# Sums of weights by transfers within DRAM ahead of their use, and token sums at an earlier step, in a two-level Strassen MLP

## The chip, the core and the metric

The kernel runs on one core of one Trainium2 chip. The metric is the device time of one execution in microseconds, the median of several runs. The core has five engines with an instruction queue each: PE (TensorE: matmul, with PEld for its weight loads), DVE (VectorE), ACT (ScalarE), POOL (GpSimd) and SP, which here only issues transfers. An engine works through its queue in order; an instruction that waits holds up all that is queued behind it. Transfers started by SP (queue q1 in the profile) and by POOL (queue q0) run on the core's 16 DMA engines. Transfers that add into their destination are started by POOL in this kernel.

## The reference, cut to what matters

One decoder block on 2048 tokens of width 1024, all in float32: attention and a gated unit side by side, merged, then an MLP. The change touches only the first matrix product of the MLP:

```
h = _rmsnorm(x, norm_pre_mlp)                        # 2048 x 1024
a = relu(einsum('bsd,df->bsf', h, w_mlp_in))         # w_mlp_in is 1024 x 4096
y = einsum('bsf,fd->bsd', a * a, w_mlp_out)
x = x + _rmsnorm(y, norm_post_mlp)
```

## The kernel before

Everything up to the MLP's normalised input `h2_d` (in DRAM) ends some 1390 us into the span. Then comes the first MLP stage (`hstep`, `hproduct`), up to about 2064 us, and the second (`yproduct`), up to the end.

**Two levels of seven products.** The first stage computes the product of the transposed weights (left) and the normalised tokens (right) with the Strassen-Winograd scheme in two levels: seven block products in place of eight, and each of them again split into seven. The outer level is a loop over the seven entries of `OUTER`, in the order A11, A12, S2, S1, S4, S3, A22: these are the left operands. The letters A11 to A22 are quarters of the weight matrix (rows by features, columns by depth), and

- S1 = A21 + A22
- S2 = S1 - A11
- S4 = A12 - S2
- S3 = A11 - A21 (the kernel before makes its negative, A21 - A11, and subtracts the product)

Each outer product runs over eight steps `q` (`HQ = 8`), so there are 56 steps `(o, q)` in `hsteps`, numbered `n`. A step takes 512 KB of left operand and makes seven inner products of six matmuls each (two blocks of depth, three matmuls each because float32 numbers are split in a high and a low part). That is 392 products; `yorder` lists them in order, and `k` counts them from 0, so an outer product spans 56 values of `k`. Products of neighbouring steps overlap a little in this order.

**What each engine does in a step.** SP loads the raw left operand (`load_ha`, line 1366). POOL makes the four inner sums of it (lines 1393, 1394, 1398, 1399 in `combine`), ACT rounds the parts to their high halves (1395, 1401, 1402, 1406), and DVE subtracts to get the low halves (1397, 1404, 1405, 1408). PE multiplies (1534). ACT or DVE evacuate PSUM to the accumulators `X` and the stage tiles `e` (1546 to 1552). SP stores finished tiles (`s_d`, `m5_d`). In the outer product S1 some tiles are added to `X` by a transfer that POOL starts (`collect`, 1567), and line 1579 takes them out again later.

**The order.** In this part the program's order is the order on each engine: after every product `k`, the entries of `todo[k]` that `later(k, ...)` has put there are issued. So `later` is the planner, by hand, and a number in it counts products. When the last product of step `n` is issued, the sums of step `n+3` are put at the next five products and the load of step `n+5` at the sixth; the sums that use this load start nine products after it.

**The left sums.** `TERMS` says of which terms a raw operand is made: S2 from A21, A22 and -A11; S1 from A21 and A22; S4 from A12 and -S2; S3 from A21 and -A11. The first term is loaded by SP into the buffer `hraw`, the second and third are added to the same buffer by accumulating transfers that POOL starts, three and six products after the load (line 1364). The negative of A11 and of S2 is made by ACT when that operand passes through (`negate`, 1379) and stored to DRAM by SP (`put`, 1384). There are two buffers `hraw`.

**The right operands.** For each outer product there are two tiles `w2r` of token blocks (`load_hb`, 1454), loaded at its predecessor's first step, eight blocks of 128x512 in all. For three of the outer products another block is subtracted from them first (`less_load` 1458, `less_sub` 1462, one of the two tiles on DVE, the other on POOL). Then `sum_w2` makes the inner sums T1, T3, T2 and T4 in place (lines 1484, 1485, 1487, 1489, twice each), and `op_w2`/`ops_hb` split the blocks into high and low parts ("spots", 1477 and the later-called subtractions that the profile books on line 1941). The two tiles are used again for the next outer product when the last split has read them.

Of the kernel before, what the change touches and what calls it, by code (L numbers as in the profile page):

```python
# [42 lines left out]
def block_kernel(ctx, tc, a, out):  # L43
# [90 lines left out]
    def dtile(shape, name):  # L134
        return dram.tile(shape, F32, name=name)
# [1210 lines left out]

    TERMS = dict(S2=("A21", "A22", "-A11"), S1=("A21", "A22"), S4=("A12", "-S2"), S3=("A21", "-A11"))

    def load_ha(n, term=0):
        o, q = hsteps[n]  # L1350
        terms = TERMS.get(OUTER[o][1], (OUTER[o][1],))
        if term >= len(terms):
            return
        name = terms[term]
        if not term:
            hraw_[n] = r4.tile([P, 4, 256], F32, name=f"hraw_{n}", tag="sraw", bufs=2)
        raw = hraw_[n].rearrange("p (f k) c -> p f (k c)", f=2)
        if name[0] == "A":
            f0, k0 = 2 * q + (16 if name[1] == "2" else 0), 4 if name[2] == "2" else 0
            src = a["w_mlp_in"][f0:f0 + 2, :, k0:k0 + 4].rearrange("f p k c -> p f (k c)")  # L1360
        else:
            src = neg_d[name[1:]][q]
        if term:
            pool.dma_start(raw, src, accum_op=OP.add)
        else:
            sp.dma_start(raw, src)

    def negate(n):

        o, q = hsteps[n]  # L1370
        name, raw = OUTER[o][1], hraw_[n]
        dst = neg_d[name][q].rearrange("p f c -> p (f c)")
        if name == "A11" and q > 1:
            z = [X[(0, 0, 8, 9, 12, 13, 14, 15)[q]]]
        else:
            z = [rx.tile([P, 512], F32, name=f"neg{n}{m}", tag="xs", bufs=4) for m in range(2)]
        w = D // len(z)
        for m, t in enumerate(z):
            act.activation(t, raw.rearrange("p k c -> p (k c)")[:, m * w:(m + 1) * w], AF.Copy, scale=-1.0)
        return [(dst[:, m * w:(m + 1) * w], t) for m, t in enumerate(z)]  # L1380

# [29 lines left out]
    def sum_ha(n):  # L1411
        w = hs_[n] = ring(n, f"hs_{n}", [P, 2, 7, 256])
        kept = negate(n) if OUTER[hsteps[n][0]][1] in neg_d else []
        yield from staged(combine(n, w, hraw_.pop(n)), kept)
# [53 lines left out]
    def key(o, m):  # L1468
        return m if o == 7 else (o, m)
# [9 lines left out]

    def sum_w2(q, part, eng=None):  # L1480

        r, e = w2r_[q], eng or pool
        if part == 0:
            e.tensor_sub(r[:, 4], r[:, 1], r[:, 0])
            e.tensor_sub(r[:, 1], r[:, 3], r[:, 1])
        if part in (1, 2):
            e.tensor_sub(r[:, 0], r[:, 3], r[:, 4])
        if part in (1, 3):
            e.tensor_sub(r[:, 2], r[:, 2], r[:, 0])
# [32 lines left out]
    def hproduct(k, n, i):  # L1522
# [22 lines left out]
        if m in (1, 5) and first:  # L1545
            act.activation(t, p, AF.Copy)  # L1546
        elif m in (2, 3) and first:
            dve.tensor_add(t, x_, p)
        elif m == 7:
            dve.tensor_sub(t, t, p)  # L1550
        else:
            dve.tensor_add(t, t, p)  # L1552
# [28 lines left out]
    def hstep(k, n, i):  # L1581
# [465 lines left out]
```

## Time and profile before

| | |
|---|---|
| median of 3 runs | 2691.23 us (2690.83 to 2695.79) |
| profiled execution | 2692.99 us, its span 2691.3 us |
| PE busy | 2580.0 us, 96% |
| first MLP stage | about 1390 to 2064 us |
| transfers of 512 KB that add into `hraw` (line 1364) | 40 |
| mean share of the DMA engines in the stage | 0.65 to 0.93 by outer product |

Engine times are busy times. A matmul's duration covers its way through the array and overlaps the next one's, so how fast PE goes is read from the distance of starts. "Idle before" is the time an engine stood before an instruction, with what released it. A wait is booked where the engine stood; what it waited for may itself have waited.

### The profile page before, as it was taken

Reading aid. Unit: us, or ns where it says so; the run is one execution under the profiler, and the core shown is the slowest. Engines: PE = TensorE matmul, PEld = TensorE weight load, DVE = VectorE, ACT = ScalarE, POOL = GpSimd, SP = SyncE. Lnnn points to the kernel's source line nnn. Section 1 sums busy time; section 2 is a strip of 40 time slices with the busy share of each in tenths; the row PEclk is TensorE's granted clock in tenths of the full one; section 3 lists DMA queues with packets and bytes.
Section 4 is the critical chain, followed back from the end, with each engine's and each line's share of the span. In section 5 each row is a group of like instructions: output and inputs, shape, how many; then the busy total and the mean of one; then the engine's idle time right before and its main releaser. Section 6 shows DMA issues by size and latency. Waiting matters only on the chain. (4 is left out here: it accounts for less than half of the span.)

```text
span 2691.3 us, 35656 instructions
## 1 busy us (share of the span) xinstructions
PE 2580.0 (96%) x12122; PEld 2140.5 (80%) x12122; DVE 1788.6 (66%) x3107; ACT 1110.7 (41%) x2342; POOL 1381.2 (51%) x1295
## 2 busy tenths in 40 slices
PE   9999999999999999999999968888899999999998
PEld 8888888888888877888887756767677888888887
DVE  5676574535434475765668756678678887788867
ACT  5213111254455445444355222433224555555555
POOL 0362354365364563101136456657698776777634
PEclk9999999999999999999999988999999999999999
DMA  8779778888888898645565786898976212222236
GB/s 318 279 246 325 269 228 291 298 278 264 295 269 239 239 319 313 224 157 180 181 240 198 199 207 141 223 250 195 263 239 190 84 52 92 88 87 86 87 110 211
DMA packets 419145, 568.70 MB, mean 211 GB/s; under 512 B 58897, under 2 KB 247569, under 8 KB 417938
## 3 DMA queue, kind: packets, MB, share of 16 engines
q1 hardware_dynamic: 386512, 491.09, 55.7%
q0 software_dynamic: 22560, 68.69, 9.9%
q10 hardware_dynamic: 9890, 6.62, 0.8%
q8 instruction: 96, 1.57, 0.2%
q14 instruction: 87, 0.71, 0.1%
HBM read 366.36 MB, written 195.76 MB: 209 GB/s over the span
## 5 line engine op out<-in xcount | busy, mean ns | idle before, releaser
L1534 PE MATMUL ha<-spot,hs 128*128 128x512 f32 x1344 | 351.8, 411 | 43.9 <-ACT e L1546 10.8
L1534 PEld LDWEIGHTS ha<-spot,hs 128*128 128x128 f32 x1344 | 266.0, 200 | 113.7 <-ACT e L1546 13.5
L1848 PE MATMUL ya<-spot,s 128*128 128x512 f32 x1344 | 324.1, 390 | 4.0 <-DVE X_yt L1856 2.1
L1848 PEld LDWEIGHTS ya<-spot,s 128*128 128x128 f32 x1344 | 252.2, 188 | 57.3 <-ACT spot L1477 2.5
L1534 PE MATMUL hc<-spot,hs 128*128 128x512 f32 x672 | 183.1, 410 | 40.7 <-DVE X_yt L1552 13.5
L1534 PEld LDWEIGHTS hc<-spot,hs 128*128 128x128 f32 x672 | 131.6, 198 | 75.9 <-DVE e L1552 12.9
L728 PE MATMUL g<-opA,spots 128*128 128x512 f32 x672 | 170.6, 398 | 1.8 <-DVE cv L760 1.8
L1848 PE MATMUL yc<-spot,s 128*128 128x512 f32 x672 | 170.5, 389 | 0.0
L728 PE MATMUL g<-opB,spots 128*128 128x512 f32 x648 | 164.6, 398 | 0.9 <-POOL spots L79 0.9
L96 PE MATMUL x<-hT_a,wq 128*128 128x512 f32 x384 | 149.7, 390 | 0.0
L97 PE MATMUL x<-hT_a,wq 128*128 128x512 f32 x384 | 149.4, 389 | 0.0
L98 PE MATMUL x<-hT_a,wq 128*128 128x512 f32 x384 | 149.4, 389 | 0.0
L1848 PEld LDWEIGHTS yc<-spot,s 128*128 128x128 f32 x672 | 126.1, 188 | 26.2
L728 PEld LDWEIGHTS g<-opA,spots 128*128 128x128 f32 x672 | 121.0, 188 | 23.9 <-issue 2.2
L79 POOL TENSOR_TENSOR spots<-gr,spots 128x512 fp32r<-128x512 f32 x98 | 128.7, 1317 | 20.8 <-DMA gr<-in_w_in_dram 7.0
L79 POOL TENSOR_TENSOR spot<-w2r,spot 128x512 fp32r<-128x512 f32 x79 | 112.3, 1444 | 45.3 <-ACT spot L71 45.3
L1712 ACT ACTIVATE sraw<-sraw 128x1024 f32<-128x1024 f32 x128 | 134.7, 1052 | 1.9 <-DMA sraw<-sd 0.2
L728 PEld LDWEIGHTS g<-opB,spots 128*128 128x128 f32 x648 | 116.7, 188 | 22.8 <-POOL spots L79 1.8
L71 ACT ACTIVATE hl<-r 128x512 fp32r<-128x512 f32 x48 | 30.4, 633 | 237.2 <-POOL r L329 89.0
L73 POOL TENSOR_SCALAR spots<-gr 128x512 fp32r<-128x512 f32 x86 | 55.4, 644 | 132.7 <-PE g L728 92.8
L978 DVE TENSOR_REDUCE o<-po 128x256 f32<-128x512 f32 x48 | 33.2, 692 | 133.9 <-PE po L977 133.9
L1397 DVE TENSOR_TENSOR hs<-hraw,hs 128x768 fp32r<-128x768 f32 x56 | 64.0, 1143 | 76.4 <-ACT hs L1395 76.4
(477 smaller groups left out, 6782.1 us busy)
## 6 DMA issues: line engine op xcount, KB each, us to landing
sraw<-sd SPq DMA_DIRECT2D x128, 256.0 KB, 3.3
hraw<-in_w_mlp_in_dram SPq DMA_DIRECT2D x56, 512.0 KB, 5.0
qk<-hl SPq DMA_DIRECT2D x24, 1024.0 KB, 5.7
qq<-qk SPq DMA_DIRECT2D x96, 256.0 KB, 5.1
sd<-e SPq DMA_DIRECT2D x64, 256.0 KB, 4.5
w2r<-in_w_mlp_out_dram SPq DMA_DIRECT2D x16, 1024.0 KB, 9.3
g<-gated SPq DMA_DIRECT2D x56, 256.0 KB, 4.9
gr<-sgd SPq DMA_DIRECT2D x53, 256.0 KB, 4.7
```

The costliest lines, as they stand in the source:

```text
L71: act.activation(hi, src, AF.Copy)
L73: pool.tensor_scalar(hi, src, 1.0, 1.0, op0=OP.mult, op1=OP.mult)
L79: (pool if lo_eng == "pool" else dve).tensor_sub(lo, src, f32(hi))
L96: pe.matmul(ps, lh, rh, start=start, stop=False)
L97: pe.matmul(ps, lh, rl, start=False, stop=False)
L98: pe.matmul(ps, ll, rh, start=False, stop=stop)
L728: pe.matmul(p, w[:, l, k], h[:, r, k], start=i in (1, 6, 5, 4) and not k and not m, stop=k == 3 and m == 2, skip_group_check=True)
L978: dve.tensor_reduce(ot[:, :, j * 64:(j + 1) * 64], po.rearrange("p (b h e) -> p b e h", b=4, h=2), axis=AX.X, op=OP.add)
L1397: dve.tensor_sub(lo[:, :3], raw[:, :3], f32(hi[:, :3]))
L1534: pe.matmul(p, w[:, l, S_AT[i], kk * P:(kk + 1) * P], b[r], start=i in (1, 2, 5) and not kk and not z, stop=kk == 1 and z == 2, skip_group ...
L1712: act.activation(sraw_[n], sraw_[n], func)
L1848: pe.matmul(p, s[:, l], w[r], start=i in (1, 2, 5) and not m and not o, stop=m == 1 and o == 2, skip_group_check=True)
```

## The change

Two things are changed, both in the first MLP stage.

The left sums are made in DRAM. There is now a DRAM tensor for each of S1, S2, S3 and S4. `negate` stores -A11 to the place of S2, and -S2 to the places of S4 and of S3. Accumulating transfers from the weights to these places (`add_rows`, started by POOL) complete them: S2 gets A21 and A22, S4 gets A12, S3 gets A22 (which makes A11 - A21, so the product is added now). S1 is first copied, A21 from DRAM to DRAM (`copy_rows`, started by SP), and then gets A22. All are placed at a fixed `k` by a loop over `q`. `load_ha` is one transfer for every operand.

The inner sums of the token blocks for the next outer product are placed from its predecessor's fourth step on (`q == 3`) in place of the sixth and seventh, with one tile on DVE and the other on POOL; T4 stays at the last step, one on each engine too. The early subtractions of `less_sub` come four products apart in place of five, the first a product earlier.

```
@@ dtile
-    neg_d = {name: dtile([NF // 4, P, 2, 512], f"neg{name}d") for name in ("A11", "S2")}
+    sums_d = {name: dtile([NF // 4, P, 2, 512], f"{name}d") for name in ("S1", "S2", "S3", "S4")}
@@ load_ha
-    TERMS = dict(S2=("A21", "A22", "-A11"), S1=("A21", "A22"), S4=("A12", "-S2"), S3=("A21", "-A11"))
+    def left_rows(name, q):
+        f0, k0 = 2 * q + (16 if name[1] == "2" else 0), 4 if name[2] == "2" else 0
+        return a["w_mlp_in"][f0:f0 + 2, :, k0:k0 + 4].rearrange("f p k c -> p f (k c)")
-        if term:
-            pool.dma_start(raw, src, accum_op=OP.add)
-        else:
-            sp.dma_start(raw, src)
+        raw = hraw_[n] = r4.tile([P, 4, 256], F32, name=f"hraw_{n}", tag="sraw", bufs=2)
+        sp.dma_start(raw.rearrange("p (f k) c -> p f (k c)", f=2), left_rows(name, q) if name[0] == "A" else sums_d[name][q])
+    def add_rows(name, q, term):
+        pool.dma_start(sums_d[name][q], left_rows(term, q), accum_op=OP.add)
+    def copy_rows(name, q, term):
+        sp.dma_start(sums_d[name][q], left_rows(term, q))
+    NEGATED = {"A11": ("S2",), "S2": ("S4", "S3")}
@@ negate
-        return [(dst[:, m * w:(m + 1) * w], t) for m, t in enumerate(z)]
+        return [(sums_d[to][q].rearrange("p f c -> p (f c)")[:, m * w:(m + 1) * w], t)
+                for to in NEGATED[name] for m, t in enumerate(z)]
@@
+    def sum_hb(q, name, eng):
+        to, x, y = {"T1": (4, 1, 0), "T3": (1, 3, 1), "T2": (0, 3, 4), "T4": (2, 2, 0)}[name]
+        r = w2r_[q]
+        eng.tensor_sub(r[:, to], r[:, x], r[:, y])
@@ hproduct
-        elif m == 7:
-            dve.tensor_sub(t, t, p)
@@ hstep
-                    later(k + 12 + 5 * m, less_load, o + 1, b)
+                    later(k + 11 + 4 * m, less_load, o + 1, b)
-                        later(k + 16 + 5 * m, less_sub, o + 1, b, kk)
+                        later(k + 15 + 4 * m, less_sub, o + 1, b, kk)
-        if i == 6 and q in (5, 6):
-            for w in range(2):
-                later(k + w, sum_w2, key(o + 1, w), 0 if q == 5 else 2, dve if not o else None)
+        if i == 6 and q == 3:
+            for m, part in enumerate(("T1", "T3", "T2")):
+                for w, eng in enumerate((dve, pool)):
+                    later(k + ((7, 11, 16) if o + 1 in LESS else (3, 8, 16))[m] + w, sum_hb, key(o + 1, w), part, eng)
-                    later(k + 3 + w, sum_w2, key(o + 1, w), 3)
+                    later(k + 3 + w, sum_hb, key(o + 1, w), "T4", (dve, pool)[w])
@@ before the loop over products
+        later(49 + 5 * q, add_rows, "S2", q, "A21")
+        later(60 + 5 * q, add_rows, "S2", q, "A22")
+        later(64 + 7 * q, copy_rows, "S1", q, "A21")
+        later(80 + 7 * q, add_rows, "S1", q, "A22")
+        later(162 + 7 * q, add_rows, "S4", q, "A12")
+        later(200 + 7 * q, add_rows, "S3", q, "A22")
@@ after the load of step m + 2
-                    if m + 2 < NH:
-                        later(k + 9, load_ha, m + 2, 1)
-                        later(k + 12, load_ha, m + 2, 2)
```

More of the change, by code (lines that the diff above doesn't have):

```diff
@@ L1345, in ring, with load_ha @@
         return (l3 if n % 3 == 2 else r4).tile(shape, F32R, name=name, tag=f"s{n % 3}")
-    TERMS = dict(S2=("A21", "A22", "-A11"), S1=("A21", "A22"), S4=("A12", "-S2"), S3=("A21", "-A11"))
-    def load_ha(n, term=0):
+    def left_rows(name, q):
+        f0, k0 = 2 * q + (16 if name[1] == "2" else 0), 4 if name[2] == "2" else 0
+        return a["w_mlp_in"][f0:f0 + 2, :, k0:k0 + 4].rearrange("f p k c -> p f (k c)")
+    def load_ha(n):
         o, q = hsteps[n]
[L1351 to L1360, printed above, removed]
-        else:
-            src = neg_d[name[1:]][q]
-        if term:
-            pool.dma_start(raw, src, accum_op=OP.add)
-        else:
-            sp.dma_start(raw, src)
+        name = OUTER[o][1]
+        raw = hraw_[n] = r4.tile([P, 4, 256], F32, name=f"hraw_{n}", tag="sraw", bufs=2)
[5 more added lines that the diff above has]
+    NEGATED = {"A11": ("S2",), "S2": ("S4", "S3")}
     def negate(n):
@@ L1371, in negate @@
         name, raw = OUTER[o][1], hraw_[n]
-        dst = neg_d[name][q].rearrange("p f c -> p (f c)")
         if name == "A11" and q > 1:
@@ L1412, in sum_ha @@
         w = hs_[n] = ring(n, f"hs_{n}", [P, 2, 7, 256])
-        kept = negate(n) if OUTER[hsteps[n][0]][1] in neg_d else []
+        kept = negate(n) if OUTER[hsteps[n][0]][1] in NEGATED else []
         yield from staged(combine(n, w, hraw_.pop(n)), kept)
@@ L1478, in ops_hb, with sum_w2 @@
             later(k + 1 + m, eng.tensor_sub, lo, src, f32(hi))
-    def sum_w2(q, part, eng=None):
-        r, e = w2r_[q], eng or pool
+    def sum_hb(q, name, eng):
+        to, x, y = {"T1": (4, 1, 0), "T3": (1, 3, 1), "T2": (0, 3, 4), "T4": (2, 2, 0)}[name]
+        r = w2r_[q]
+        eng.tensor_sub(r[:, to], r[:, x], r[:, y])
+    def sum_w2(q, part):
+        r, e = w2r_[q], pool
         if part == 0:
@@ L1485, in sum_w2 @@
             e.tensor_sub(r[:, 1], r[:, 3], r[:, 1])
-        if part in (1, 2):
+        else:
             e.tensor_sub(r[:, 0], r[:, 3], r[:, 4])
-        if part in (1, 3):
             e.tensor_sub(r[:, 2], r[:, 2], r[:, 0])
```

## The prediction

> **What bounds the kernel now.** I read the page first, then the waits, then the first MLP stage (1390 to 2064 us) product by product.
>
> ```profile
> span 2691.3 us, 35656 instructions
> PE 2580.0 (96%) x12122; PEld 2140.5 (80%) x12122; DVE 1788.6 (66%) x3107; ACT 1110.7 (41%) x2342; POOL 1381.2 (51%) x1295
> ...
> L1534 PE MATMUL ha<-spot,hs 128*128 128x512 f32 x1344 | 351.8, 411 | 43.9 <-ACT e L1546 10.8
> ...
> L1534 PE MATMUL hc<-spot,hs 128*128 128x512 f32 x672 | 183.1, 410 | 40.7 <-DVE X_yt L1552 13.5
> ```
>
> TensorE sets the time, and 84.6 us of its idle time of 111 stand before the products of this one stage (line 1534), behind evacuations of PSUM. The next rows cut the stage at its seven outer products, A11, A12, S2, S1, S4, S3, A22, which I call phases 0 to 6 (cut where the first evacuation of each form appears). The columns are the stretch, its length, the busy time of PE, PEld, DVE, ACT and POOL, the granted clock, the DMA engines' share, GB/s.
>
> ```profile
> 1390.00:1472.00 82.00, 79.73 (x356) 64.84 (x355) 65.48 (x93) 51.87 (x98) 46.55 (x45) 1.00 0.76 267
> 1472.00:1558.00 86.00, 78.75 (x330) 64.55 (x331) 68.14 (x95) 22.30 (x42) 44.44 (x46) 0.94 0.65 180
> 1558.00:1675.00 117.00, 87.43 (x316) 67.47 (x316) 67.52 (x95) 30.65 (x59) 63.79 (x64) 0.85 0.73 175
> 1675.00:1777.00 102.00, 88.77 (x365) 70.51 (x363) 73.52 (x89) 44.49 (x84) 74.67 (x72) 0.95 0.87 216
> 1777.00:1867.00 90.00, 81.39 (x336) 64.76 (x336) 70.82 (x101) 24.80 (x45) 57.30 (x58) 0.96 0.93 239
> 1867.00:1965.00 98.00, 83.63 (x335) 66.41 (x336) 69.87 (x99) 25.49 (x47) 69.94 (x65) 0.93 0.82 231
> 1965.00:2064.00 99.00, 85.71 (x352) 67.08 (x351) 78.13 (x104) 31.60 (x54) 93.79 (x79) 0.97 0.72 222
> ```
>
> Undisturbed, a product of six matmuls takes 1.36 us, so a phase of 56 products takes 76.2 us:
>
> ```profile
> 1429.22 1.52 PE L1534 MATMUL hc<-spot,hs 128*128 128x512 f32 x6
> 1430.58 1.52 PE L1534 MATMUL hb<-spot,hs 128*128 128x512 f32 x6
> ```
>
> Above that floor stand 10, 41, 26, 14, 22 and 23 us in phases 1 to 6: 136 us, idle time and the lower clock after it (0.85 in phase 2) together. No engine fills phase 2; it waits in a chain. The longest stall of it, in order of time:
>
> ```profile
> 1589.19 0.90 POOL L1364 DMA_DIRECT2D hraw<-negA11d  x1 [4.85 <-DMA hraw<-in_w_mlp_in_dram]
> 1596.65 1.15 ACT L1379 ACTIVATE neg<-hraw 128x512 f32<-128x512 f32 x2 [11.63 <-DMA hraw<-negA11d]
> 1598.56 0.96 DVE L1397 TENSOR_TENSOR hs<-hraw,hs 128x768 fp32r<-128x768 f32 x1 [10.43 <-ACT hs L1395]
> 1599.44 0.68 DVE L1552 TENSOR_TENSOR X_yt<-X_yt,hc 128x512 f32<-128x512 f32 x1
> 1600.17 2.93 PE L1534 MATMUL hc<-spot,hs 128*128 128x512 f32 x6 [9.53 <-DVE X_yt L1552]
> ```
>
> POOL stands 4.85 us until the second term has landed before it may issue the third, ACT waits for the third, DVE for ACT, and the evacuation that frees the PSUM bank is queued behind DVE's operand. Three chained transfers do not fit into the nine products (12 us) between a load and its use. The waits of the stage say the same in sum:
>
> ```profile
> ACT hs L1406 <- POOL hraw L1399: 159.7, 53, 7.3
> POOL fifth L1393 <- DMA hraw<-negA11d: 42.3, 11, 6.7
> POOL hraw L1364 <- DMA hraw<-in_w_mlp_in_dram: 40.6, 12, 5.3
> SPq L1366 <- DVE hs L1408: 204.9, 41, 11.3
> ```
>
> **The change, part by part.** I write k for the index of a product in the order of the stage (56 per phase).
>
> Removed: the 40 accumulations into the load buffer and their waits on the step's path. Each operand of S2, S1, S4, S3 is now one 512 KB load, as in phases 0 and 1. What that gives shows in phase 1: after its first product it ran without a stall until the first chained operand at its end:
>
> ```profile
> 1550.43 2.93 PE L1534 MATMUL hc<-spot,hs 128*128 128x512 f32 x6 [6.18 <-DVE e L1552]
> ```
>
> Added: the same 40 accumulations, each within DRAM, from k=49 to k=249, at places fixed by the loop over q. Issues:
>
> ```profile
> L1364 POOL DMA_DIRECT2D hraw<-in_w_mlp_in_dram x16: 1196/1218/1248, 1532.8 to 1741.3; - x16
> L1364 POOL DMA_DIRECT2D hraw<-negA11d x16: 866/898/926, 1539.0 to 1930.8; - x16
> L1384 SPq DMA_DIRECT2D negS2d<-neg x16: 319/323/688, 1547.6 to 1660.9; - x16
> ...
> 1532.76 1.25 POOL L1364 DMA_DIRECT2D hraw<-in_w_mlp_in_dram  x1
> 1533.55 1.23 POOL L1398 TENSOR_TENSOR hraw<-fifth,hraw 128x256 f32<-128x256 f32 x1
> ```
>
> All 40 now read rows of the weights, so 24 of them go from about 0.89 to 1.22 us (8 us of POOL's issue time in all); POOL goes on 0.79 us after such an issue. SP gets 16 more stores at 0.32 us (the negated S2 goes to two places) and 8 copies; its queue waits 205 us for buffers in this stage anyway, so I cost these at nothing; were that cover gone, 24 issues cost 8 us of SP.
>
> The price of the transfers themselves, from the queues' shares in phases 1, 2, 3, and of the plain queue in 4 and 5 (packets, MB, share of all 16 engines):
>
> ```profile
> q1 hardware_dynamic: 17134, 13.82, 53.1%
> ...
> q0 software_dynamic: 3011, 7.54, 39.8%
> q1 hardware_dynamic: 8450, 12.92, 33.2%
> ...
> q0 software_dynamic: 3961, 7.92, 46.4%
> q1 hardware_dynamic: 6995, 14.07, 39.9%
> ...
> q1 hardware_dynamic: 18394, 16.41, 57.8%
> ...
> q1 hardware_dynamic: 22251, 19.41, 63.6%
> ```
>
> Phase 2: 39.8% of 117 us for 7.54 MB is 3.24 us of all engines per accumulation of 0.524 MB; a plain transfer 33.2% of 117 for 12.92 MB, 1.57 us. No row shows an accumulation within DRAM. Its bounds are 1.57 us (as a plain transfer) and 6.5 us (twice today's). I take 3.24, the same operation with another end.
>
> Phase 1 (k 56 to 111) takes the brunt: 19 accumulations (A21 and A22 for S2, A22 for S1) and 7 copies. The second term of S2 must wait for the first to land, eleven products (15 us) after it was issued, and this wait stands on POOL, with the sums of line 1393 to 1399 queued behind it and ACT and DVE behind those. From k=49 to the last such wait at k=95 are 46 products, 62.6 us. By then 15 accumulations (49 us), 5 copies (8 us) and the phase's own plain traffic (53.1% of 86 us, 39 of 56 products, 32 us) want the engines for 89 us. 12 us of it can lag, the distance of a load from its use. The other 14 us stand on POOL and reach PE: phase 1 takes 76+14 = **90**, 4 more than now.
>
> The Trainium skill speaks against the change here (DMA: Bandwidth & Descriptors, "Issuing engines are not separate DMA queues"): transfers started by any engine run on the same 16 engines and interleave. By it, moving a transfer ahead saves none of its engine time, and the 8 copies and 16 stores are added load; the first rival below gives the time. The same page ("Two DMAs through the same engine are not ordered") asks for a semaphore wait between dependent transfers, which is the POOL wait of phase 1; the trace agrees, since line 1364 waits today.
>
> Phase 2: no accumulation into a buffer, 3 to 4 in DRAM; plain 39 us plus 12 for the doubled stores and 13 for accumulations and a copy's rest, of some 80. DVE's 67.5 us stay. Floor 76, what spills over from phase 1 another 6: **82**, 35 less.
>
> Phase 3: POOL becomes the bound. Its 74.7 us, less 4 inner sums (6 us, below), plus 11 accumulations and some 15 collects at 0.8 and 0.6 us of queue: 87 us. DMA: plain 41, collects of 0.262 MB 24 (half of 3.24 each), 11 accumulations 36 make 100, of which a part lags into phase 4. **91**, 11 less.
>
> Phase 4: DVE 70.8+2.7 and no chained loads; the lag of phase 3: **84**, 6 less. Phase 5: **86**, 12 less, of which the next part is half.
>
> The inner sums of the token blocks: per phase eight TENSOR_TENSOR, six of them on POOL at products 5 and 6 of 8, where the next phase's operands are split; now from the fourth step on, half on DVE.
>
> ```profile
> L1484 POOL TENSOR_TENSOR hb<-hb x10: 1284/1598/2021, 1524.8 to 1940.1; 128x512 f32<-128x512 f32 x10
> L1462 DVE TENSOR_TENSOR hb<-hb x12: 678/744/1182, 1604.2 to 1923.8; 128x512 f32<-128x512 f32 x12
> ...
> 1945.85 0.72 POOL L1393 TENSOR_TENSOR fifth<-hraw 128x256 f32<-128x256 f32 x1
> 1946.61 0.42 ACT L1401 ACTIVATE hs<-fifth 128x256 fp32r<-128x256 f32 x1 [7.13 <-POOL fifth L1393]
> ...
> 1949.18 2.93 PE L1534 MATMUL ha<-spot,hs 128*128 128x512 f32 x6 [4.56 <-DVE X_gpost L1550]
> ```
>
> Four sums of 1.6 us and two of line 1579 ran on POOL from 1940 to 1946, ACT stood 7.13 us and PE 4.56. POOL loses 4 x 1.6 = 6.4 us a phase, DVE gains 4 x 0.74 = 3.0. DVE then has 70 to 77 us of work in phases 1 to 5, hidden under 76 of products only just; if that cover goes, 3 us a phase, 18 in all, come back. The nearer spacing of the early subtractions (line 1462) moves them by at most four products and costs nothing by itself.
>
> Phase 6: POOL's 93.8 us less 6.4: 88, plus what waits at the change of stage: **91**, 8 less.
>
> Sum: +4 -35 -11 -6 -12 -8 = -68 us. The profiled execution took 2692.99 us, 1.7 outside its span of 2691.3 and 1.8 over the median of 2691.23. 2693-68 = 2625, and against the median **2623 us**. With the accumulation at 1.57 us phase 1 takes 78, phase 3 its 87 of POOL: 2607. At 6.5 us phase 1 takes 15 x 6.5 + 40 - 75 = 63 us of standing, 139 in all, and phases 3 and 4 together want 217 us of the engines where 175 are there and 24 can go to phase 5: 18 more. -68+49+18 is about 0.
>
> **Rivals.** First, the DMA engines become the bound. Their demand over phases 1 to 5 is 118 (plain 46, copies 11, accumulations 61), 65, 100, 68 (plain 52, 4 accumulations and 2 collects 16) and 62 us (plain), 413 in all; the forecast gives them 433, a share of 0.95, and no phase has shown more than 0.93. At 0.90 these phases take 459 instead of 493: with phase 6, -42, **2649**. For it: 0.87 and 0.93 in phases 3 and 4. Against: deadlines are now 40 products off, so a backlog may stand.
>
> Second, on the other side: an accumulation within DRAM is dear, and POOL stands at its wait in phase 1. It decides from 6.5 us on; at 8 us phase 1 takes 161, phases 3 and 4 grow by 40 over the forecast: -68+71+40 = +43, **2734**. For it: today's accumulation already costs twice a plain transfer. Against: the price is the same at rows of 2 and 4 KB.
>
> Third, everything hides: 78, 78, 87, 78, 80, 88 for phases 1 to 6 against 592 now, -103, **2588**. For it: phases 0 and 1 show that single loads leave no stall.
>
> Fourth, it doesn't do what it says: if slices of one DRAM tensor were held apart only as a whole, each second term would wait for a first term issued one product before, 8 waits of some 5 to 6 us more in phase 1: **2666**. Against: no wait of SP on a DRAM tensor's other slices shows today.
>
> **How the numbers follow.** Forecast 0.48, DMA bound 0.22, dear accumulation 0.08, all hidden 0.17, whole tensors 0.05. A measurement tells about 0.2% (5 us) from no change. Slower is the second rival, 0.08; no change 0.04, the worst part of the first; faster 0.88. The range, 2585 to 2672, takes in the forecast, the third and fourth rival and most of the first, and leaves out the second.
>
> **What would show it.** Right: phase 2 near 80 us at a clock near 1, no wait of ACT on a load over 5 us, POOL's longest waits at the second terms of S2 between k=85 and 95, phases 3 and 6 with POOL over 0.9. Wrong: phase 1 over 100 us, accumulations of more than 5 us of the engines, DVE waiting for token blocks at its new sums, or phase 2 still over 95.

## The result and the profile after

The changed kernel took **2661.32 us** in the median of its runs (2658.79 to 2662.44), against 2691.89 us (2690.83 to 2695.79) for the kernel before on the same chip: a ratio of 0.9883 [0.9865, 0.99], 30.6 us faster. The forecast was 2623 us, a gain of 68. In the runs beside the experiments below, the kernel before took 2690.5 to 2699.0 us, so a few us between single runs mean nothing.

These are the lines of the page that answer to the first fence of the prediction (the matmul line is 1536 now).

```profile
span 2657.1 us, 35689 instructions
...
PE 2566.7 (97%) x12122; PEld 2129.8 (80%) x12122; DVE 1822.1 (69%) x3129; ACT 1113.1 (42%) x2342; POOL 1361.1 (51%) x1273
...
L1536 PE MATMUL ha<-spot,hs 128*128 128x512 f32 x1344 | 343.9, 402 | 58.4 <-DVE e L1550 29.5
...
L1536 PE MATMUL hc<-spot,hs 128*128 128x512 f32 x672 | 178.7, 403 | 8.6 <-DVE e L1552 8.2
```

TensorE's idle time ahead of the hc products fell from 40.7 to 8.6 us: most of the stalls at the late operands are gone, as meant. Ahead of the ha products it rose from 43.9 to 58.4, and half of that, 29.5 us, now waits for line 1550 to write its result tile e. Before, the wait at the same place in the code (line 1548 there) was 8.6 us. Of the 29.5 us, 19.5 lie in the second outer product and 9.5 in the fifth. The next view cuts the stage exactly at the first product of each outer product, phases 0 to 6 (columns as in the prediction: stretch, length, PE, PEld, DVE, ACT, POOL, granted clock, DMA share, GB/s).

```profile
1389.30:1463.40 74.10, 73.29 (x329) 59.99 (x328) 61.67 (x86) 46.36 (x87) 47.60 (x46) 1.00 0.82 286
1463.40:1576.60 113.20, 86.65 (x338) 67.74 (x337) 73.34 (x99) 29.02 (x55) 55.53 (x60) 0.90 1.00 247
1576.60:1665.50 88.90, 81.15 (x339) 64.47 (x338) 78.18 (x104) 32.78 (x61) 56.94 (x55) 0.97 0.75 229
1665.50:1754.30 88.80, 81.19 (x338) 64.90 (x337) 77.73 (x86) 38.42 (x72) 62.72 (x65) 0.96 0.93 227
1754.30:1846.30 92.00, 81.42 (x338) 63.28 (x337) 78.15 (x107) 28.63 (x54) 53.58 (x54) 0.98 0.91 244
1846.30:1930.20 83.90, 78.00 (x337) 62.53 (x336) 74.18 (x104) 24.08 (x45) 57.26 (x53) 1.00 0.75 227
1930.20:2029.50 99.30, 90.07 (x377) 70.58 (x376) 86.80 (x111) 34.19 (x60) 94.32 (x77) 0.98 0.75 230
```

Phase 1 has a DMA share of 1.00 over its whole length. TensorE is idle in 26.5 of its 113.2 us, and at a granted clock of 0.90 it is busy for 8.7 us more than in phase 5 at 1.00. The table puts the phases of all kernels of this case side by side, in us, each cut in its own trace at the start of the first product of each outer product (the last one ends at the start of the stage's last product).

| kernel | stage starts | 1 | 2 | 3 | 4 | 5 | 6 |
|---|---|---|---|---|---|---|---|
| before | 1390.7 | 87.9 | 123.0 | 93.2 | 92.2 | 98.7 | 104.6 |
| forecast | | 90 | 82 | 91 | 84 | 86 | 91 |
| after | 1389.3 | 113.2 | 88.9 | 88.8 | 92.1 | 83.9 | 99.2 |
| e1_no_s1 | 1396.4 | 101.8 | 81.7 | 86.0 | 91.8 | 83.9 | 98.6 |
| e1_thin_s1 | 1391.0 | 98.7 | 85.2 | 91.4 | 91.9 | 82.8 | 98.2 |
| e2_far_second | 1389.5 | 113.8 | 90.8 | 90.1 | 92.0 | 84.4 | 97.6 |
| e3_left_only | 1391.6 | 115.3 | 84.1 | 88.5 | 91.3 | 85.3 | 104.5 |
| e4_token_only | 1391.0 | 84.7 | 120.6 | 89.7 | 94.3 | 94.4 | 98.8 |
| e5_s1_early | 1405.2 | 100.5 | 81.6 | 88.2 | 92.0 | 85.2 | 97.3 |
| e6_s2_from_s1 | 1399.5 | 86.2 | 82.2 | 89.3 | 92.8 | 82.7 | 98.3 |
| e7_spread | 1404.9 | 84.0 | 95.2 | 81.5 | 94.5 | 83.8 | 99.3 |
| e8_wide_rows | 1392.5 | 109.8 | 89.6 | 87.9 | 93.2 | 83.5 | 99.6 |
| e9_m5_early | 1389.8 | 116.1 | 89.4 | 88.0 | 93.7 | 85.0 | 101.7 |
| e10_no_m5 | 1402.5 | 84.7 | 85.3 | 91.3 | 92.3 | 85.5 | 96.9 |
| e10_together | 1403.1 | 83.6 | 85.3 | 86.1 | 91.2 | 86.3 | 101.6 |

How far such lengths scatter can be read from the table itself. The last two kernels issue the same instructions up to product 300, yet phase 3 takes 91.3 us in one and 86.1 in the other. In the nine kernels without an edit ahead of the stage, the start lies between 1389.3 and 1396.4 us.

So the change gained 34.1 us in phase 2 and 14.8 in phase 5, some 10 more in phases 3 and 6 together, and paid 25.3 of it back in phase 1. What filled phase 1 shows in the transfers there. First the queues and the issues of the kernel before in its phase 1 (queue: packets, MB, share of all 16 engines; issue: count, size, median us to landing):

```profile
q1 hardware_dynamic: 16240, 13.37, 49.4%
q0 software_dynamic: 584, 1.39, 10.1%
...
sd<-e SPq DMA_DIRECT2D x26, 256.0 KB, 4.5
hraw<-in_w_mlp_in_dram SPq DMA_DIRECT2D x8, 512.0 KB, 3.9
```

The same view of the changed kernel, 1463 to 1577 us:

```profile
q0 software_dynamic: 5440, 10.49, 52.1%
q1 hardware_dynamic: 18551, 17.55, 47.7%
...
S2d<-in_w_mlp_in_dram POOLq DMA_DIRECT2D x16, 512.0 KB, 9.4
sd<-e SPq DMA_DIRECT2D x26, 256.0 KB, 10.3
...
hraw<-in_w_mlp_in_dram SPq DMA_DIRECT2D x6, 512.0 KB, 10.5
```

The additions within DRAM (q0) hold the 16 engines for 52.1% of 114 us, 59.4 us, and the plain transfers beside them for another 54.4 us. Together these are the phase. 10.49 MB are 20 additions of 0.524 MB, so one costs 2.97 us. The 26 stores of tile e, which have nothing to do with the change, land after 10.3 us in place of 4.5. The waits of the phase (in total, times, longest) say who pays for that:

```profile
ACT hs L1403 <- POOL hraw L1396: 33.5, 9, 8.4
DVE e L1550 <- DMA sd<-e: 26.0, 7, 8.2
...
PE ha L1536 <- DVE e L1550: 19.5, 8, 5.9
...
ACT hs L1392 <- DMA hraw<-in_w_mlp_in_dram: 17.5, 3, 13.0
...
POOL S2d L1358 <- issue: 6.0, 2, 5.2
POOL S1d L1358 <- issue: 2.4, 2, 1.6
```

VectorE stands 26.0 us because a result tile is still being stored, TensorE 19.5 us behind VectorE, ScalarE 17.5 us for loads. POOL's standing before an addition, which the forecast had made the price of this phase, is only 8.4 us (the last two lines; "issue" means that the profile shows nothing it waited for). One stall behind the stores, in order of time (start, length, instruction, and in brackets the wait ahead of it):

```profile
1490.72 7.46 SPq L1948 DMA_DIRECT2D sd<-e  x2
...
1498.22 4.67 SPq L1451 DMA_DIRECT2D hb<-tqd  x1
...
1501.77 0.69 DVE L1550 TENSOR_TENSOR e<-X_yt,ha 128x512 f32<-128x512 f32 x1 [8.21 <-DMA sd<-e]
...
1502.51 2.93 PE L1536 MATMUL ha<-spot,hs 128*128 128x512 f32 x6 [5.76 <-DVE e L1550]
```

SP spends 7.46 us on issuing two stores and 4.67 on one load, where an issue of a store took 0.3 us in the prediction's rows. VectorE's next result finds no free tile e for 8.21 us (the tiles come from two rings of four buffers), so PSUM isn't emptied, and TensorE stands for 5.76.

### The profile page after: what moved, and what is told of

Same layout as the page of the kernel before. It is cut to its first block, busy times and chain, and to the rows that moved or that the text cites. A ratio compares the mean times of both kernels' runs of the same rounds, so it can differ in the third digit from the quotient of the medians.

```text
span 2657.1 us, 35689 instructions
## 1 busy us (share of the span) xinstructions
PE 2566.7 (97%) x12122; PEld 2129.8 (80%) x12122; DVE 1822.1 (69%) x3129; ACT 1113.1 (42%) x2342; POOL 1361.1 (51%) x1273
## 5 line engine op out<-in xcount | busy, mean ns | idle before, releaser
L1536 PE MATMUL ha<-spot,hs 128*128 128x512 f32 x1344 | 343.9, 402 | 58.4 <-DVE e L1550 29.5
L1536 PEld LDWEIGHTS ha<-spot,hs 128*128 128x128 f32 x1344 | 254.7, 192 | 130.0 <-DVE e L1550 29.9
L73 POOL TENSOR_SCALAR wq<-wq_r 128x1024 fp32r<-128x1024 f32 x24 | 31.7, 1328 | 138.3 <-PE va L98 87.9
```

The costliest lines, as they stand in the source:

```text
L73: pool.tensor_scalar(hi, src, 1.0, 1.0, op0=OP.mult, op1=OP.mult)
L1536: pe.matmul(p, w[:, l, S_AT[i], kk * P:(kk + 1) * P], b[r], start=i in (1, 2, 5) and not kk and not z, stop=kk == 1 and z == 2, skip_group ...
```

## The experiments

The theory after the result: **phase 1 lasts as long as its transfers hold the 16 engines**, and the plain stores carry that to TensorE through the tiles e. Rivals: POOL standing at the second terms of S2 (the step of the forecast), or the additional issues on SP and POOL.

**S1's transfers taken out of phase 1.** The left operand of S1 is loaded as A21 alone, so S1's second term is left out of what is computed. In the first kernel its copies and additions are gone, in the second they are still issued, on 16 of 128 partitions.

```diff
e1_no_s1
...
-        later(64 + 7 * q, copy_rows, "S1", q, "A21")
-        later(80 + 7 * q, add_rows, "S1", q, "A22")
e1_thin_s1
...
+        n = 16 if name == "S1" else P
-        pool.dma_start(sums_d[name][q], left_rows(term, q), accum_op=OP.add)
+        pool.dma_start(sums_d[name][q][:n], left_rows(term, q)[:n], accum_op=OP.add)
...
-        sp.dma_start(sums_d[name][q], left_rows(term, q))
+        sp.dma_start(sums_d[name][q][:16], left_rows(term, q)[:16])
```

> The changed kernel without the making of S1: no copies, no additions to them; the load of S1 reads the rows of A21 from the weights instead (so the sum S1 is left out of the computation). Theory A, load: phase 1 of the changed kernel (114 us, DMA share 0.98) is as long as its transfers keep the 16 engines busy, and the plain stores feed back through the stage tiles e, for which DVE waits. Then taking away 7 copies of 1.57 us and 5 additions of 2.9 us brings phase 1 to 86 to 92 us and the execution to about 2636 us. Theory B, waits: the time goes to waits that the change added on POOL (a second term for its first). S1 has 2.4 us of those in phase 1, so about 2658 us. Theory C, issues: POOL and SP lose time to the added instructions; then as A.

> As the run without S1, but the 8 copies and 8 additions are still issued at their places, each over 16 of the 128 partitions (an eighth of the bytes; their result isn't used, S1 is loaded from A21). Theory A, load: within 5 us of the run without S1, about 2639 us, since an eighth of the bytes is 3 us of the engines. Theory C, issues: as the changed kernel, 2661 us, because every instruction is still there.

Measured: 2643.55 us without them, 2642.57 us with thin ones (one run each): about 18 us less either way, so it is the bytes that cost, not the issues. Phase 1 without S1's transfers is 101.8 us, though, where the theory gave 86 to 92. The engines' share there is 0.93, so they are held for 95 us, and VectorE still waits 26.4 us for its result tiles: 7 us of the phase aren't the engines' time. Phase 1 of the thin version, its length and its queues:

```profile
1465.10:1563.70 98.60, 81.64 (x337) 64.17 (x336) 68.58 (x98) 27.76 (x52) 53.87 (x59) 0.97 0.98 234
```

```profile
q0 software_dynamic: 4544, 8.65, 51.4%
q1 hardware_dynamic: 16946, 14.49, 46.1%
...
sd<-e SPq DMA_DIRECT2D x26, 256.0 KB, 7.7
```

The engines' time fell from 113.8 to 97.5% of 99, 96.5 us, 17 less; the phase is 14.5 us shorter and its share still 0.98. Phase 2 falls too, from 88.9 to 81.7 and 85.2 us. In the changed kernel, one copy and four additions of S1 are issued in phase 2 itself, so how much of this is their time and how much a backlog from phase 1 isn't told apart.

**The second terms of S2 farther from the first.** The addition of A22 is issued 22 products after that of A21 in place of 11.

```diff
-        later(60 + 5 * q, add_rows, "S2", q, "A22")
+        later(71 + 5 * q, add_rows, "S2", q, "A22")
```

> The changed kernel with the second terms of S2 at 71 + 5q in place of 60 + 5q, 22 products behind the first terms in place of 11, so that POOL needn't wait for them. The same transfers in the same phase. Theory A, load: phase 1 still 108 us or more, 2655 to 2665 us. Theory B, waits: POOL's 6 us at these transfers and what queues behind them go, 2645 to 2652 us.

Measured: 2661.71 us (one run), nothing gained. The phase and POOL's waits in it:

```profile
1463.60:1577.40 113.80, 83.06 (x337) 65.91 (x336) 73.36 (x99) 28.95 (x55) 54.31 (x59) 0.90 1.00 241
```

```profile
POOL S2d L1358 <- issue: 5.5, 2, 3.4
...
POOL S1d L1358 <- issue: 0.7, 1, 0.7
```

POOL stands 5.5 us at S2's additions with the first terms issued twice as far back, against 6.0 before. So the first term isn't what it stood for, and the rival from the forecast's step falls. The changed kernel's own rows fit: its additions land after 9.4 us in the median, and the forecast had put 15 us between the two terms.

**The two parts of the change, each alone.** First the left sums without the new places of the token blocks' inner sums, then the inner sums (and the nearer spacing of their loads) in the kernel before.

```diff
e3_left_only: the changed kernel with
+        if i == 6 and q in (5, 6):
+            for w in range(2):
+                later(k + w, sum_w2, key(o + 1, w), 0 if q == 5 else 2, dve if not o else None)
-        if i == 6 and q == 3:
...
-                    later(k + ((7, 11, 16) if o + 1 in LESS else (3, 8, 16))[m] + w, sum_hb, key(o + 1, w), part, eng)
...
e4_token_only: the kernel before with the same lines the other way round
```

> The left sums in DRAM alone; the inner sums of the token blocks and the early subtractions as in the kernel before. By the forecast's own terms the moved token sums were worth some 18 us in phases 3 to 6, so this one would take about 2679 us. Rival: with DVE at 76 to 85 us of work in phases of 76 us of products the moved sums are worth nothing or cost their 3 us a phase; then 2645 to 2661 us.

> The kernel before with the moved inner sums of the token blocks (and the early subtractions) alone; left sums added in the load buffer as before. The left sums alone took 2666.9 us, both parts 2661.3, so the moved sums are worth 5.5 us beside the new left sums. If the parts add, 2688 us. If the moved sums take out stalls at the ends of phases that the new left sums take out too, more: 2675 to 2683 us. By the forecast's terms (18 us) 2675.

Measured: left sums alone 2666.86 us, ratio 0.9906 [0.989, 0.9923]; token sums alone 2676.63 us, ratio 0.993 [0.9913, 0.9947]. The left sums lie between the two expectations for them (2679, and 2645 to 2661); the token sums lie in the range for parts that take out the same stalls. By these ratios the parts are worth 25 and 19 us alone, 44 in sum, and together they give 31: 13 us less. By the table, the sum of the two gains exceeds the joint gain by 7 us in phase 2, 4 in phase 3 and 3 in phase 5. Token sums alone take 2.4 to 5.8 us from phases 1, 2, 3, 5 and 6 and add 2.1 to phase 4. Beside the left sums only phase 6 shows them clearly (104.5 to 99.2), and phase 2 is 4.8 us longer with them than without; why isn't shown. Phase 1 without the left sums is 84.7 us, so all of its growth is theirs. Phase 6 of the kernel before, and then that of the kernel with the token sums alone, shows the size of the move itself:

```profile
1960.30:2064.80 104.50, 91.21 (x376) 71.66 (x375) 83.40 (x108) 34.61 (x60) 99.21 (x83) 0.97 0.70 216
```

```profile
1948.80:2047.60 98.80, 89.58 (x376) 70.42 (x375) 86.33 (x111) 33.94 (x59) 93.99 (x77) 0.98 0.76 231
```

POOL does 5.2 us less, VectorE 2.9 more (forecast: 6.4 and 3.0 a phase).

**S1 made ahead of the stage, and then S2 made from it.** In the first kernel S1's copies and additions move before the first MLP stage, into the loop over output blocks of the attention's projection. In the second, S2 (which is A21 + A22 - A11, so S1 - A11) also gets one addition, of S1, in place of two. The second kernel also has S1's rows in DRAM 520 elements apart, not 512.

```diff
e5_s1_early
+            if n in (1, 2):
+                with behind():
+                    copy_rows("S1", 4 * n + i - 4, "A21")
+            if (n, i) > (1, 0) and n < 3 or (n, i) == (3, 0):
+                with behind():
+                    add_rows("S1", 4 * n + i - 5, "A22")
...
-        later(64 + 7 * q, copy_rows, "S1", q, "A21")
-        later(80 + 7 * q, add_rows, "S1", q, "A22")
e6_s2_from_s1, on top of that
...
-        later(49 + 5 * q, add_rows, "S2", q, "A21")
-        later(60 + 5 * q, add_rows, "S2", q, "A22")
+        later(60 + 5 * q, add_rows, "S2", q, "S1")
```

> The changed kernel with the 8 copies and 8 additions of S1 ahead of the stage, between the blocks of rows of the attention's output (one per block). Theory A, load: phase 1 as without S1, 100 to 104 us, phase 2 at 82; ahead of the stage the engines have a share of 0.5 to 0.8, so the moved 36 us cost 0 to 8 us there: 2642 to 2650 us. If it were S1's place in the queues and not its bytes, nothing changes here against the run without S1 either.

> As with S1 ahead of the stage, and S2 gets the finished S1 in one addition (8 in phase 1 at 60 + 5q) in place of A21 and A22 (16). Theory A, load: phase 1 of the run without S1 wanted the engines for 95 us (0.93 of 101.8); 8 additions of 3.1 us less leave 70 us, under the 76 us of the products, so the phase falls to 77 to 84 us and the execution to 2618 to 2630 us. If something else than the load held phase 1 (the sums on DVE in the middle of the phase), it stays at 95 us or more, and the execution above 2638.

Measured: 2653.9 and 2634.9 us (one run each). Both are slower than expected. The first version gains 12.7 us in phase 1 and 7.3 in phase 2, as forecast, but loses 15.9 before the stage starts, where 0 to 8 were allowed. The second takes eight additions, some 24 us of the engines, out altogether, and phase 1 drops to 86.2 us, below that of the kernel before but above the 77 to 84 expected. Its row, queues and wait:

```profile
1474.10:1560.30 86.20, 79.75 (x337) 63.33 (x336) 70.58 (x99) 28.71 (x55) 42.63 (x48) 0.98 0.83 214
```

```profile
q1 hardware_dynamic: 16800, 14.16, 52.5%
q0 software_dynamic: 2176, 4.19, 30.1%
```

```profile
DVE e L1553 <- DMA sd<-e: 9.4, 3, 3.3
```

The engines' share is 0.83, and VectorE's wait for its result tiles falls from 26.0 to 9.4 us. The landing of those stores (8.6 us) is still nearly twice that of before: a slow store holds VectorE only when no buffer of its ring is free.

Length by share gives the engines' time in phase 1 of each kernel. A share of 1 alone says only that they never stood; that they set the length shows where bytes were taken out of a full phase (thin S1: 17 us less for the engines, 14.5 us less for the phase). Where it is 113 us (the changed kernel), 110 (the wide rows below) or 97 (thin S1), the phase lasts as long, within 2 us. Where it is 95 (no S1, S1 early), 72 (S2 from S1) or 52 (before), the phase takes 101.8, 100.5, 86.2 and 87.9 us, 6 to 12 us more than the engines' time or the 76.2 us of the products, whichever is longer. So the theory holds while the engines are full; what the 6 to 12 us are stays open.

**The additions of S4 and S3 moved.** On top of that kernel, S4's come 42 products earlier and S3's 22 later.

```diff
-        later(162 + 7 * q, add_rows, "S4", q, "A12")
-        later(200 + 7 * q, add_rows, "S3", q, "A22")
+        later(120 + 7 * q, add_rows, "S4", q, "A12")
+        later(222 + 7 * q, add_rows, "S3", q, "A22")
```

> As the one before, and the additions to S4 at 120 + 7q (phase 2, where the engines have a share of 0.66), those to S3 at 222 + 7q (from the end of phase 3 through phase 4). Theory A: phase 3, with 0.93 of its 88.8 us in the changed kernel, loses some 30 us of demand and falls to 80 to 85 us; phase 4 (0.91) gains 9 us of demand and phase 2 23 us, both still under 1: 2612 to 2626 us. If POOL and not the DMA engines holds phase 3, it stays near 88.

Measured: 2647.24 us (one run), 12 more, where 9 to 23 less were expected; 5 of the 12 lie ahead of the stage, where nothing was changed. Phases 2 and 3 of it:

```profile
1563.50:1658.70 95.20, 82.41 (x339) 65.12 (x338) 81.77 (x104) 33.92 (x63) 60.29 (x58) 0.95 0.76 217
1658.70:1740.20 81.50, 78.16 (x338) 63.95 (x337) 74.14 (x86) 39.69 (x74) 54.43 (x57) 0.98 0.80 210
```

Phase 3 loses 7.8 us and phase 2 takes up 13.0, at a share of only 0.76. The fall of phase 3 fits a phase held by its transfers, but that isn't shown: the scatter there is 5 us, and the last two kernels below have four of S4's additions fewer in phase 3 and take 91.3 and 86.1 us. Phase 2 has a stall that S2 from S1 lacks, in order of time:

```profile
1624.90 0.69 DVE L1462 TENSOR_TENSOR hb<-hb 128x512 f32<-128x512 f32 x1 [7.86 <-DMA hb<-h2d]
...
1627.25 0.67 DVE L1555 TENSOR_TENSOR X<-X,ha 128x512 f32<-128x512 f32 x1
...
1627.98 2.93 PE L1539 MATMUL ha<-spot,hs 128*128 128x512 f32 x6 [7.88 <-DVE X L1555]
```

VectorE stands 7.86 us at an early subtraction (`less_sub`) whose token block hasn't landed, the evacuation queued behind it comes late, and TensorE stands 7.88 us. In the whole phase VectorE waits 12.3 us for token blocks, against 2.6 with S2 from S1. So a mean share of 0.76 doesn't keep a single load from coming late.

**Rows of 2 KB for the stores.** The stores of tile e write one row of 2 KB per partition in place of four of 512 B; the second stage then computes on elements in another order.

```diff
-        later(k + 2, sp.dma_start, s_d[fq, half][:, :, {(0, 0): 0, (1, 0): 1, (1, 1): 2, (0, 1): 3}[f, c]],
-              t.rearrange("p (i c) -> p i c", i=4))
+        later(k + 2, sp.dma_start, s_d[fq, half][:, {(0, 0): 0, (1, 0): 1, (1, 1): 2, (0, 1): 3}[f, c]].rearrange("p i c -> p (i c)"), t)
```

> The changed kernel, with one thing different: the first stage's plain stores of its results (256 KB each, tile e) go to DRAM in rows of 2 KB in place of four rows of 512 B per partition. The bytes and the count of transfers stay; the second stage then reads its operands in another order of elements, so what it computes isn't the reference's. Theory A (the 16 DMA engines' time alone sets the first-product phase, whatever the row size): the stores cost little less, phase 1 stays 111 to 114 us, total 2657 to 2662. Theory B (packets of the two queues are taken in turn, so that short rows starve beside the additions' longer ones): the stores' landing in phase 1 falls from 10.3 us to 6 to 7 us, VectorE's wait for the result tile from 26 us to under 12 us, phase 1 is 95 to 105 us, total 2640 to 2652.

Measured: 2659.53 us (one run). Phase 1 and its transfers:

```profile
1466.70:1576.50 109.80, 85.95 (x337) 66.36 (x336) 68.07 (x99) 28.98 (x55) 54.55 (x60) 0.92 1.00 255
```

```profile
DMA packets 14078, 28.22 MB, mean 248 GB/s; under 512 B 1098, under 2 KB 1098, under 8 KB 14073
...
q1 hardware_dynamic: 8633, 17.66, 44.4%
...
sd<-e SPq DMA_DIRECT2D x26, 256.0 KB, 13.4
```

With fewer than half the packets, the plain queue takes 50.6 us in place of 54.4, and the phase is 3.4 us shorter, a little under the 111 to 114 of theory A and far over the 95 to 105 of theory B. The stores land no sooner (13.4 against 10.3 us), and VectorE's wait for its result tiles is 21.9 us, where theory B had under 12. So theory B falls: short rows aren't starved by long ones here.

**m5 earlier.** The last phase is the one in which POOL is busy 94.3 of 99.3 us. The loads and subtractions of m5 start at product 308 in the changed kernel, in the middle of phase 5, and then come 9.5 products apart. Here they start at product 300, 8 apart, so they move by 8 to 18 products (the expectation below has their old place wrong).

```diff
-        t = 7 * (5 * HQ + 4) + 19 * q // 2
+        t = 300 + 8 * q
```

> The changed kernel, with the loads and subtractions of m5 (the 40 of the last phases) put at product 300 + 8 q instead of at the last phase's start on, so that POOL has more of the stage for them. Theory (POOL, busy 94.3 us of the last phase's 99.2, holds that phase): the last phase falls to 90 to 94 us, the one before it rises from 83.9 to 86 to 90, total 2655 to 2658. Rival (transfers or TensorE's own rate hold it): the last phase stays 98 to 100 us, total 2661 or more.

Measured: 2667.95 us (one run), 6.6 more; 2.9 of that lie in phase 1, ahead of the edit. The last phase:

```profile
1936.10:2037.80 101.70, 91.74 (x379) 71.89 (x378) 85.58 (x113) 35.33 (x62) 89.15 (x76) 0.97 0.68 213
```

POOL has 5.2 us less to do, and the phase is 2.4 us longer. So taking work from POOL doesn't shorten it, and this theory falls, my forecast's reason for phase 6 with it. ScalarE's waits for the sums on POOL (lines 1390 and 1396) come to 51 us in the changed kernel and 53 in this one, which would fit an order of POOL's work that is wrong rather than too much of it; no run here tests that.

**Two more moves, each version timed in four runs.** On top of S2 from S1: S1's transfers one output block earlier, S4's additions from product 140 on; then the same with m5 from product 300 on.

```diff
e10_no_m5
-            if n in (1, 2):
+            if n in (0, 1):
...
+            if n in (1, 2):
...
-        later(162 + 7 * q, add_rows, "S4", q, "A12")
+        later(140 + 7 * q, add_rows, "S4", q, "A12")
e10_together, on top of that
-        t = 7 * (5 * HQ + 4) + 19 * q // 2
+        t = 300 + 8 * q
```

> The version in which S1 is made ahead of the stage and S2 gets a single addition from S1 (the one that took 2634.9 us), with S1's copies and additions one output block earlier, and S4's additions at product 140 + 7 q instead of 162 + 7 q. m5 stays where it is. Theory (the stage takes as long as its transfers where they are crowded, and those ahead of the stage find free engines if they are early enough): the stage starts at 1390 to 1395 us instead of 1399.5, the phase lengths stay as there, phase 3 loses 3 to 5 us; total 2620 to 2632. Rival (the transfers ahead of the stage cost that earlier stage what they take, wherever they lie): start stays 1398 to 1403, total 2634 to 2640.

> The kernel of the run before this one (S1 ahead of the stage one block earlier, S2 from S1, S4 at 140 + 7 q), with m5's loads and subtractions at 300 + 8 q as well. If POOL holds the last phase: another 3 to 6 us less than that kernel. If it does not: within 2 us of it.

Measured: 2641.24 us (2640.09 to 2642.72), ratio to the kernel before **0.9806 [0.979, 0.9822]**, and with m5 2645.85 us, 0.9823 [0.9809, 0.9838]. The first beats both kernels, the changed one by 20 us. Its own expectation (2620 to 2632) failed all the same: the single run of S2 from S1 took 2634.9, so the two moves aren't shown to help. The stage starts at 1402.5 us, as the rival had it and as late as with S1 one block later, and phase 3 gained nothing (91.3). The price of S1's transfers ahead of the stage, in the changed kernel and then in this one:

```profile
1300.00:1350.00 50.00, 50.00 (x235) 41.65 (x234) 34.20 (x65) 20.64 (x40) 7.49 (x11) 1.00 0.66 228
```

```profile
1300.00:1350.00 50.00, 45.86 (x210) 37.73 (x209) 30.19 (x61) 16.72 (x34) 12.72 (x17) 0.97 0.80 235
```

TensorE, without a gap in this stretch, now has gaps of 4.1 us in it, at a share of 0.80. The stage starts 6 to 13 us later than in the kernels without these transfers ahead of it, and the phases behind it spare more than that. m5 early gave nothing here either (4.6 us more in all, phase 6 at 101.6 against 96.9), which agrees with the run before.

## Why the prediction was right or wrong, point by point

**Phase 1, forecast 90, measured 113.2: this is the step that failed.** I set 89 us of transfers, wanted by product 95, against 62.6 us, let 12 lag, and put "the other 14 us" on POOL. The count was short: the 15 additions leave out three of S1's, at products 80, 87 and 94, some 10 us. The price was right (2.97 us for an addition where 3.24 was taken), and so was the demand: the first rival has 118 us for phase 1, and the engines were held 113.8. What failed is the path by which a surplus reaches TensorE, and with it the amount that can lag. A phase with 118 us of transfers can't end after 90 unless 28 us of them lag, and I had let 12. I never set the phase's own demand against its own length, though both stood in the text. Nor does lag stay with the additions, whose results nobody needs soon: the plain stores of tile e stand in the same engines, behind them VectorE (26.0 us), and behind VectorE TensorE (19.5 us). POOL's waits, on which my 14 us stood, were 8.4 us, and doubling the distance to the first terms changed nothing. I had weighed a rule of the Trainium skill (DMA: Bandwidth & Descriptors, "Issuing engines are not separate DMA queues"): transfers run on the same 16 engines and interleave, whichever engine starts them. The trace agrees: in phase 1 the queue of POOL has 52.1% of the engines and that of SP 47.7%, together all of them.

**Phase 2, forecast 82, measured 88.9.** The main gain, 34.1 us, is where and nearly as large as forecast. In three versions without S1's transfers in phases 1 and 2 (no S1, S1 early, S2 from S1), phase 2 takes 81.6 to 82.2 us, so the 7 us above the forecast go with those transfers. Whether it is the backlog of phase 1 or their own time in phase 2 isn't told apart, and the token sums have a part: the left sums alone take 84.1 us.

**Phase 3, forecast 91, measured 88.8, for the wrong reason.** POOL was to be the bound with 87 us; it is busy 62.7. Part of that was the base: my cuts, at evacuations, gave this phase 102 us before where its products give 93.2. And the 74.7 us of POOL in that window already held the issues of 14 collects and 8 additions, so the sum counts the collects twice and doesn't take out the additions that went. The DMA share of 0.93, and the fall to 81.5 us where the additions of S4 and S3 were moved out, fit transfers as the bound; the two last kernels don't bear it out, so it stays open.

**Phase 4, forecast 84, measured 92.1.** It did not move. The five additions issued in it, its collects and the lag of phase 3 came to 28.8% of 92 us, 26.5 us of q0, at a share of 0.91 in all:

```profile
q1 hardware_dynamic: 18066, 17.84, 62.2%
q0 software_dynamic: 2435, 4.59, 28.8%
```

None of the kernels, the one before included, took it under 91 us. Its waits name token blocks that land late (VectorE 6.5 us and POOL 12.8 us at line 1459, POOL 4.7 before), and TensorE stands 9.5 us behind line 1550; no run tests this, and what holds the phase stays open.

**Phase 5, forecast 86, measured 83.9**: right in length, but not in its parts. Half of the gain was to come from the inner sums; the left sums alone give 13.4 of the 14.8 us, the inner sums alone 4.3. **Phase 6, forecast 91, measured 99.2**: the inner sums gave 5.4 us where 8 were forecast. "POOL 88 plus the change of stage" fails, since POOL isn't its bound; what is stays open.

**The sum.** By the lengths as measured, the forecast missed by +23.2, +6.9, -2.2, +8.1, -2.1 and +8.2 us, 42.1 in all. The phases before were 599.6 us by exact cuts where my windows had 592, so the forecast lengths would have been worth 75.6 us, and 33.5 is what the phases gave; the spans differ by 34.2. The medians differ by 30.6, because the profiled execution of before lay 1.1 us over its median and that of after 2.5 under.

**The rivals.** Nearest in mechanism is the first, the DMA engines as the bound, with 413 us of demand in phases 1 to 5. Measured, length by share: 113 + 67 + 83 + 84 + 63 = 410. By phase the demand came otherwise than forecast (phase 3 had 83 of its 100, phase 4 had 84 where 68 were set). Its time, 2649, was 12 us short: 8 us because it let the engines run at 0.90 throughout, where over these 467 us they ran at 0.88, full in phase 1 and at 0.75 in phases 2 and 5, and the rest in phase 6 and the base. The fourth rival's 2666 lies nearer, but by another mechanism, and POOL's waits at second terms (6.0 us, two of them) speak against its eight waits of 5 to 6 us. The dear addition is excluded by 2.97 us, the third rival (everything hides) by phase 1.

**What I had named as signs.** Phase 1 over 100 us was the one that spoke against me, and it came, with a wait of ScalarE on a load of 13.0 us where none over 5 was to be. POOL's longest wait was not at a second term of S2 (5.2 us) but for a load (11.3 us), and of phases 3 and 6 only the latter had POOL over 0.9 (0.71 and 0.95). Additions of more than 5 us and waits at the new sums did not come. Phase 2 at 89 and a clock of 0.97 lies between right and wrong. That VectorE's added work of 3 us a phase stayed hidden isn't shown: phase 2 is 4.8 us longer with the token sums than without them.

## What to carry to other kernels

Before moving transfers ahead, add up, phase by phase, how long all transfers hold the DMA engines and set each sum against the phase's own length: where it is more, expect the phase to grow to that sum, as phase 1 did here (118 us by the first rival's sum, 113.2 measured), however far off the moved transfers' own deadlines are, because unrelated stores and loads stand in the same engines. A sum that fits is no promise: a single late load cost 7.9 us at a share of 0.76. Then look for the sum that needs fewer transfers (S2 from S1, worth 19 us beyond S1's move in single runs, 14 of them in phase 1) before looking for better places. And cut a stage at its products when phases are to be compared: the cut at evacuations made phase 3 of the kernel before 9 us too long.

## What the runs showed of the hardware that was not expected

- An accumulating transfer within DRAM costs the engines 2.97 us per 512 KB with the engines full (3.24 us at a share of 0.83, with S2 from S1: 30.1% of 86 us for 4.19 MB). That is no more than one from DRAM into SBUF (3.24 us in the prediction's rows), and still nearly twice a plain transfer (1.63 us, 54.4 us for 17.55 MB).
- With the engines full, an issue on SP took up to 4.67 us for a load and 7.46 us for two stores (0.3 us for one otherwise), so what stands behind it in SP's queue is issued that much later.
- Stores in rows of 512 B and in rows of 2 KB differ little: 54.4 us for 17.55 MB of the plain queue against 50.6 us for 17.66 MB, 7.5% by the MB, and no earlier landing.
